# An eight-core encoder layer: token tiles of 384 to 512 in place of 256, and weights cast by DMA into the weight ring

## The chip, the cores and the metric

One Trainium2 chip, all 8 cores. Each core takes two of 16 prompt streams (2 x 2048 tokens) and two of 16 decode streams (2 x 32 tokens); nothing is exchanged between cores. The metric is the device time of the slowest core, in microseconds (us). In some executions the cores of one die, or of both, run at a lower granted clock; such runs are called slow here and are not used for comparisons.

## The reference

One layer: an input projection into six parts, a recurrent branch (conv, gates, scan), a spatial gating branch, a merge with an output projection, and a SwiGLU feed-forward network (FFN). Cut to what matters:

```python
xn = rmsnorm(x, g_pre_mix)
xa, ga, u, v, gates = split(xn @ w_in)            # 1024 -> 6 x 1024
xc, conv_new = causal_conv(xa, conv_prev, conv_w, conv_b)     # width 4
hseq, h_last = rglru(xc, h0, w_a, b_a, w_x, b_x, lam)         # scan over time
o_a = (hseq * gelu(ga)) @ w_br_a
o_b = (gelu(u) * spatial_gate(layernorm(gelu(v)), w_s, b_s)) @ w_br_b
mix = (sigmoid(g_a) * o_a + sigmoid(g_b) * o_b) @ w_out
x   = x + rmsnorm(mix, g_post_mix)
hn  = rmsnorm(x, g_pre_ffn)
gate, up = split(hn @ w_ffn_in)                   # 1024 -> 2 x 2816
x   = x + rmsnorm((silu(gate) * up) @ w_ffn_out, g_post_ffn)
```

## The kernel before

It works in 16 tiles of 256 prompt tokens and one tile of 64 decode tokens. The weights (69 pieces of 128 x 2048) stream through a ring of eight slots, once for each tile. At the start Pool issues casts of the float32 weights into a bfloat16 copy in DRAM, and SP loads the ring from that copy:

```python
TT = 256
...
def rec_cvt(pid):                                  # float32 DRAM -> bfloat16 DRAM
    P.op("pool", lambda e, ...: e.dma_start(out=dst[:, :, c0:c0 + n], in_=src), writes=[("wsc", pid)], ...)
...
    P.op("sp", lambda e, ...: e.dma_start(out=wring[:, slot, :], in_=wsc[pid, :, :]),
         reads=[("wsc", pid)], writes=[("wr", slot)], ...)
```

Mixer and FFN are lists of stages with costs. The FFN of a tile lies 0.35 of a tile behind the next mixer's start, so old FFN work stands beside the start of every mixer. The conv's result, the input of the gates, has a buffer for each of the eight channels:

```python
F_OFFSET = 0.35
...
allst += [(t, 0, i, f) for i, (t, f) in enumerate(timed(mixer_stages(ti), float(ti)))]
allst += [(t, 1, i, f) for i, (t, f) in enumerate(timed(ffn_stages(ti), ti + 1.0 + F_OFFSET))]
...
def s_gate(c):
    P.op("pe", lambda e: e.matmul(ps[:, bg_, 0:ntok], lhsT=wab[:, c, :], rhs=xcb[:, c, 0:ntok], ...),
         reads=[("wab",), ("xcb", c)], ...)
```

Of the kernel before, what the change touches and what calls it, by code (L numbers as in the profile page):

```python
# [6 lines left out]
F32 = mybir.dt.float32  # L7
# [5 lines left out]
D = 1024  # L13
# [6 lines left out]
TT = 256  # L20
NSLOT = 8
CV_AHEAD = 24
INTERLEAVE = True
F_OFFSET = 0.35
FOUT_W = 1.0
# [11 lines left out]

class _Cell:
    __slots__ = ("w", "r")

    def __init__(self):
        self.w = None
        self.r = []

class Prog:
# [47 lines left out]
    def emit(self, block, eng_sems, final_waits):  # L93
        cnt = {e: 0 for e in self.ENGS}
        dcnt = {}
        for e in self.ENGS:
            for o in self.ops[e]:
                if o.dma_sem is not None:
                    k = id(o.dma_sem)
                    dcnt[k] = dcnt.get(k, 0) + 16  # L100
                    o.tok = (o.dma_sem, dcnt[k])
                elif o.needed:
                    cnt[e] += 1
                    o.tok = (eng_sems[e], cnt[e])
        self.final_dma = dcnt
# [31 lines left out]
def build_program(n_prompt_tiles=SEQ // TT, do_sample=True, sample_first=False):  # L137
# [9 lines left out]
    xs_in = din("xs", [2, DEC, D])  # L147
    sh_in = din("sh", [2, D])
    sc_in = din("sc", [2, 3, D])
    g_pre_mix = din("g_pre_mix", [D])  # L150
    w_in = din("w_in", [D, 6 * D])
    conv_w = din("conv_w", [4, D])
    conv_b = din("conv_b", [D])
    w_a = din("w_a", [16, 64, 64])
    b_a = din("b_a", [D])
    w_x = din("w_x", [16, 64, 64])
    b_x = din("b_x", [D])
    lam = din("lam", [D])
    w_br_a = din("w_br_a", [D, D])
    ln_g = din("ln_g", [D])  # L160
    ln_b = din("ln_b", [D])
    w_s = din("w_s", [8, 128, 128])
    b_s = din("b_s", [8, 128])
    w_br_b = din("w_br_b", [D, D])
    w_out = din("w_out", [D, D])
    g_post_mix = din("g_post_mix", [D])
    g_pre_ffn = din("g_pre_ffn", [D])
    w_ffn_in = din("w_ffn_in", [D, 2 * DFF])
    w_ffn_out = din("w_ffn_out", [DFF, D])
    g_post_ffn = din("g_post_ffn", [D])  # L170

    yp = dout("yp", [2, SEQ, D])
    ys = dout("ys", [2, DEC, D])
    hp = dout("hp", [2, D])
    cp = dout("cp", [2, 3, D])
    hs_o = dout("hs", [2, D])
    cs_o = dout("cs", [2, 3, D])
    vs_o = dout("vs", [2, DEC, D])

    pieces = []  # L180

    def add_piece(kc, ncols, srcs):
        pieces.append(dict(kc=kc, ncols=ncols, srcs=srcs))
        return len(pieces) - 1

    def colblk(w, c0, n):
        return w[:, c0:c0 + n].rearrange("(k p) n -> p k n", p=128)

    WIN = [add_piece(8, 256, [(colblk(w_in, cb * 256, 256), 0, 256)]) for cb in range(24)]
    BRA = [add_piece(8, 256, [(colblk(w_br_a, h * 256, 256), 0, 256)]) for h in range(4)]  # L190
    BRB = [add_piece(8, 256, [(colblk(w_br_b, h * 256, 256), 0, 256)]) for h in range(4)]
    WOUT = [add_piece(8, 256, [(colblk(w_out, h * 256, 256), 0, 256)]) for h in range(4)]
    FING = [add_piece(8, 256, [(colblk(w_ffn_in, q * 256, 256), 0, 256)]) for q in range(NFF // 2)]
    FINU = [add_piece(8, 256, [(colblk(w_ffn_in, DFF + q * 256, 256), 0, 256)]) for q in range(NFF // 2)]
    FOUT = [add_piece(2, 1024, [(w_ffn_out[r * 256:(r + 1) * 256, :].rearrange("(k p) n -> p k n", p=128), 0, 1024)])
            for r in range(NFF // 2)]
    NPIECE = len(pieces)
    PSZ = 2048
    wsc = nc.dram_tensor("wsc", [NPIECE, 128, PSZ], BF16).ap()

    tiles = []
    for b in range(2):
        for tt in range(n_prompt_tiles):
            tiles.append(dict(kind="p", b=b, tt=tt, ntok=TT, nsub=TT // 128, PT=128,
                              first=(tt == 0), last=(tt == n_prompt_tiles - 1)))
    if do_sample:
        st = dict(kind="s", ntok=64, nsub=1, PT=64, first=True, last=True)
        if sample_first:
            tiles.insert(0, st)
        else:  # L210
            tiles.append(st)
    NT = len(tiles)

    with contextlib.ExitStack() as es:
# [7 lines left out]
        xbuf = [sb(f"xbuf{i}", [128, 2, D]) for i in range(3)]  # L222
        xsb = [sb(f"xsb{i}", [128, D], BF16) for i in range(2)]
        junk = sb("junk", [128, D], BF16)
        xnTs = [sb(f"xnT{i}", [128, NCH, TT], BF16) for i in range(2)]
        hnT = sb("hnT", [128, NCH, TT], BF16)
        tok = [sb(f"tok{i}", [128, D]) for i in range(2)]
        XAW = TT + 4
        xaT = sb("xaT", [128, NCH, XAW])
        xcf = sb("xcf", [128, NCH, TT])  # L230
        xcb = sb("xcb", [128, NCH, TT], BF16)
        chTr = [sb(f"chTr{i}", [128, TT]) for i in range(2)]
        chTi = [sb(f"chTi{i}", [128, TT]) for i in range(4)]
        chA = [sb(f"chA{i}", [128, TT]) for i in range(4)]
        chE = [sb(f"chE{i}", [128, TT]) for i in range(4)]
        chH = [sb(f"chH{i}", [128, TT]) for i in range(2)]
        gga = sb("gga", [128, NCH, TT])
        hgT = sb("hgT", [128, NCH, TT], BF16)
        gu = sb("gu", [128, NCH, TT])
        gsT = sb("gsT", [128, NCH, TT], BF16)  # L240
        gv = [sb(f"gv{i}", [128, D]) for i in range(2)]
        vn = [sb(f"vn{i}", [128, D], BF16) for i in range(2)]
        Tsig = sb("Tsig", [128, 2, TT])
        t2 = sb("t2", [128, NCH, TT], BF16)
        tmpA2 = sb("tmpA2", [128, 2, TT])
        mixT = sb("mixT", [128, NCH, TT], BF16)
        sgt = [sb(f"sgt{i}", [128, TT]) for i in range(2)]
        ffT = sb("ffT", [128, NFF, TT], BF16)
        hst = sb("hst", [128, NCH, 2])
        stats = sb("stats", [128, 96])  # L250
        st6 = [sb(f"st6_{i}", [128, 4, 6]) for i in range(2)]
        mvt = [sb(f"mvt{i}", [128, 2]) for i in range(2)]
        identf = sb("identf", [128, 128])
        identb = sb("identb", [128, 128], BF16)
        nhalf = sb("nhalf", [128, 1])
        ones128 = sb("ones128", [128, 128], BF16)
        gT_pm = sb("gT_pm", [128, NCH])
        gT_pf = sb("gT_pf", [128, NCH])
        cw = sb("cw", [128, NCH, 4])
        cbT = sb("cbT", [128, NCH])  # L260
        ba2 = sb("ba2", [128, NCH])
        bx2 = sb("bx2", [128, NCH])
        lamT = sb("lamT", [128, NCH])
        cneg = sb("cneg", [128, NCH])
        hcn = sb("hcn", [128, NCH])
        wab = sb("wab", [128, NCH, 128], BF16)
        wxb = sb("wxb", [128, NCH, 128], BF16)
        wsT = sb("wsT", [128, 8, 128], BF16)
        wsS0 = sb("wsS0", [64, 8, 32], BF16)
        wsS1 = sb("wsS1", [64, 8, 32], BF16)  # L270
        bs128 = sb("bs128", [128, 8, 128], BF16)
        gbc_lng = sb("gbc_lng", [128, D])
        gbc_lnb = sb("gbc_lnb", [128, D])
# [5 lines left out]
        psh = ps[:].rearrange("p b (h c) -> p (b h) c", h=2)  # L279

        eng_sems = {e: sem("s_" + e) for e in Prog.ENGS}
        cvt_sems = [sem(f"cv{i}") for i in range(16)]
        ring_sems = [sem(f"rg{i}") for i in range(NSLOT)]
        xl_sems = [sem(f"xl{i}") for i in range(3)]
        y_sems = [sem(f"yo{i}") for i in range(3)]
        c_sems = [sem(f"cst{i}") for i in range(8)]
        so_sem = sem("sto")
        vs_sem = sem("vso")
        block = es.enter_context(nc.Block())

# [4 lines left out]
        stream_log = []  # L295

        def record(P, dry):
            stream = stream_log
            c_ctr = [0]

            def cdma(fn, reads=(), writes=()):
                i = c_ctr[0] % len(c_sems)
                c_ctr[0] += 1
                return P.op("sp", fn, reads=reads, writes=writes, dma_sem=c_sems[i], serial=True)
# [4 lines left out]
            def fb(b):  # L309
                return [("ps", 2 * b), ("ps", 2 * b + 1)]  # L310

            def _touch(b):
                lru.remove(b)
                lru.append(b)

            def alloc_bank():
                for b in lru:
                    if b not in held:
                        _touch(b)
                        return b  # L320
                raise RuntimeError("no free PSUM bank")

            def alloc_half():
                return 2 * alloc_bank()

            def alloc_pair():
                best = None
                for b in range(0, 8, 2):
                    if b in held or (b + 1) in held:
                        continue  # L330
                    age = max(lru.index(b), lru.index(b + 1))
                    if best is None or age < best[0]:
                        best = (age, b)
                if best is None:
                    raise RuntimeError("no free PSUM bank pair")
                b = best[1]
                held.add(b)
                held.add(b + 1)
                _touch(b)
                _touch(b + 1)  # L340
                return b

            def release_pair(b):
                held.discard(b)
                held.discard(b + 1)
                _touch(b)
# [801 lines left out]
```

## Time and profile before

| | before |
|---|---|
| time, median of the first three runs | 2843.87 us (2837.72 to 2921.96) |
| span of the profiled run, slowest core | 2827.5 us |
| one tile of 256 tokens in the middle | 144.1 us (1873 us for 13 tiles) |
| TensorE busy in that stretch | 1706.53 of 1873 us |

PE is TensorE's matmuls, PEld its weight loads, DVE VectorE, ACT ScalarE, POOL GpSimd, SP the core that issues most DMA. The prediction below shows most of the views. Two lines more of the waits of TensorE matter later (what waited, for what, us in all, times, longest): L721 is the gate matmul of before.

```profile
PE ps L721 <- DVE ffT L1033: 32.2, 28, 2.5
...
PE ps L721 <- ACT gga L715: 5.4, 2, 4.4
```

It waits for an FFN block to be done, 1.15 us on average, or for a gelu. The list has no wait of it for its own input, the conv result.

### The profile page before, as it was taken

What the parts mean: (1) busy time and instruction counts of PE and PEld (TensorE: products, weight loads), DVE (VectorE), ACT (ScalarE), POOL (GpSimd) and SP (SyncE); (2) the same over time, 40 slices, a digit from 0 to 9 for tenths busy, and PEclk for the clock granted to TensorE, in tenths of its full rate; (3) what the DMA queues carried; (4) which work ended last, traced back from release to release, by engine and by line L of the source; (5) the groups of instructions that cost most, each with busy time, mean ns of one, the idle gap of its engine ahead of it and who ended that gap; (6) DMA issues with size and microseconds to landing.
All of it is one profiled execution on the core that took longest, in us unless ns stands there. A gap on an engine that the chain in (4) does not pass through costs nothing.

```text
span 2827.5 us, 54756 instructions; the slowest of 8 cores (2805.4 to 2827.5 us)
## 1 busy us (share of the span) xinstructions
PE 2208.4 (78%) x18580; PEld 1756.3 (62%) x18580; DVE 1282.0 (45%) x2588; ACT 1170.9 (41%) x2206; POOL 528.0 (19%) x614
## 2 busy tenths in 40 slices
PE   0041856579899999989989999999989898986585
PEld 0031645358686767676768686767677777774363
DVE  0022432154645455555555555545464646461341
ACT  0052341152636363545445454545353636261421
POOL 2102310220303030303030303030212121211101
PEclk9985977889999999999999999999999999998797
DMA  7997999988888787887778787877878787874787
GB/s 92 156 181 106 243 183 216 189 258 274 271 263 277 252 270 267 274 269 267 264 253 279 252 282 261 274 263 268 276 260 277 252 278 257 281 245 152 242 304 267
DMA packets 264388, 692.41 MB, mean 245 GB/s; under 512 B 41794, under 2 KB 102242, under 8 KB 264116
## 3 DMA queue, kind: packets, MB, share of 16 engines
q1 hardware_dynamic: 200804, 652.72, 69.7%
q0 software_dynamic: 63312, 36.18, 12.3%
q8 instruction: 156, 2.56, 0.4%
q14 instruction: 116, 0.95, 0.1%
HBM read 707.61 MB, written 53.54 MB: 269 GB/s over the span
## 4 chain that ended last, share of the span: by engine, by line
PE 59%; DVE 10%; another core or an unknown queue 9%; DMA 8%; issue 5%; POOL 5%; ACT 3%; SPq 1%; DVEq 0%; POOLq 0%; ACTq 0%
PE ps L1022 22%; PE ps L578 21%; PE ps L1048 8%; DMA wring<-wsc 6%; PE ps L935 4%; PE ps L790 3%; DMA xaT<-sc 2%; DVE xcf L695 1%; POOL stats L417 1%; DVE tok L596 1%; POOL wsc L373 1%; DVE chH L763 1%; DVE chTi L740 1%; POOL gv L818 1%
## 5 line engine op out<-in xcount | busy, mean ns | idle before, releaser
L1022 PE MATMUL ps<-hnT,wring 128*128 128x256 bf16 (+1 forms) x5984 | 712.8, 281 | 126.4 <-DMA wring<-wsc 44.3
L1022 PEld LDWEIGHTS ps<-hnT,wring 128*128 128x128 bf16 x5984 | 586.4, 103 | 227.0 <-issue 140.7
L578 PE MATMUL ps<-xnT,wring 128*128 128x256 bf16 (+1 forms) x5440 | 633.7, 272 | 39.8 <-DVE tok L596 15.5
L578 PEld LDWEIGHTS ps<-xnT,wring 128*128 128x128 bf16 x5440 | 517.9, 100 | 134.5 <-issue 55.5
L1030 DVE SCALAR_TENSOR_TENSOR sgt<-sgt,ps 128x256 f32<-128x256 f32 (+1 forms) x374 | 151.5, 405 | 563.3 <-PE ps L1022 327.6
L1048 PE MATMUL ps<-wring,ffT 128*128 128x512 bf16 (+1 forms) x1452 | 347.0, 388 | 56.0 <-DMA wring<-wsc 49.0
L1028 ACT ACTIVATE sgt<-ps 128x256 f32<-128x256 f32 (+1 forms) x374 | 131.8, 375 | 510.0 <-PE ps L1022 406.9
L1048 PEld LDWEIGHTS ps<-wring,ffT 128*128 128x128 bf16 (+1 forms) x1452 | 142.6, 100 | 213.0 <-issue 77.9
L695 DVE SCALAR_TENSOR_TENSOR xcf<-xaT,cw,xcf 128x256 f32<-128x256 f32 (+1 forms) x408 | 192.8, 473 | 44.1 <-DVE xcf L695 1.9
L414 POOL TENSOR_SCALAR stats<-stats 128x1 f32<-128x1 f32 x165 | 39.1, 237 | 850.2 <-ACT junk L527 572.5
L918 POOL TENSOR_TENSOR mixT<-tmpA,t 128x512 bf16<-128x512 f32 (+1 forms) x68 | 76.3, 1122 | 611.5 <-PE ps L1022 330.3
L527 ACT ACTIVATE junk<-xbuf 128x1024 bf16<-128x1024 f32 (+1 forms) x66 | 69.7, 1056 | 291.5 <-DMA xbuf<-xp 199.2
L935 PE MATMUL ps<-wring,mixT 128*128 128x256 bf16 (+1 forms) x1056 | 132.0, 287 | 52.5 <-POOL mixT L918 49.8
L1033 DVE SCALAR_TENSOR_TENSOR ffT<-sgt,ps 128x256 bf16<-128x256 f32 (+1 forms) x374 | 153.0, 409 | 40.0 <-DVE sgt L1030 1.4
L601 POOL TENSOR_TENSOR xbuf<-xbuf,tok 128x1024 f32<-128x1024 f32 (+1 forms) x66 | 156.4, 2390 | 20.8 <-DVE tok L596 20.8
L706 ACT ACTIVATE xcb<-xcf 128x256 bf16<-128x256 f32 (+1 forms) x136 | 55.2, 406 | 247.9 <-DVE xcf L695 247.8
L935 PEld LDWEIGHTS ps<-wring,mixT 128*128 128x128 bf16 (+1 forms) x1056 | 107.7, 103 | 74.4 <-issue 57.7
L578 PE MATMUL ps<-hgT,wring 128*128 128x256 bf16 (+1 forms) x1088 | 124.9, 268 | 17.3 <-DVE hgT L774 11.8
L790 PE MATMUL ps<-wring,xnT 128*128 128x256 bf16 (+1 forms) x1056 | 128.6, 276 | 12.2 <-DMA wring<-wsc 8.7
L578 PE MATMUL ps<-gsT,wring 128*128 128x256 bf16 (+1 forms) x1088 | 126.4, 270 | 7.2 <-DVE gsT L883 6.3
L691 DVE TENSOR_SCALAR xcf<-xaT,cw,cbT 128x256 f32<-128x256 f32 (+1 forms) x136 | 54.4, 400 | 170.2 <-ACT xaT L686 121.8
L790 PEld LDWEIGHTS ps<-wring,xnT 128*128 128x128 bf16 (+1 forms) x1056 | 104.0, 99 | 40.3 <-issue 16.8
(112 smaller groups left out, 2599.7 us busy)
## 6 DMA issues: line engine op xcount, KB each, us to landing
wring<-wsc SPq DMA_DIRECT2D x1173, 512.0 KB, 5.5
xbuf<-xp SPq DMA_DIRECT2D x16, 1024.0 KB, 7.8
yp<-xbuf SPq DMA_DIRECT2D x32, 512.0 KB, 3.0
wsc<-w_in POOLq DMA_DIRECT2D x24, 512.0 KB, 67.9
wsc<-w_ffn_in POOLq DMA_DIRECT2D x22, 512.0 KB, 84.6
wsc<-w_ffn_out POOLq DMA_DIRECT2D x11, 512.0 KB, 70.9
wsc<-w_br_b POOLq DMA_DIRECT2D x4, 512.0 KB, 63.4
wsc<-w_br_a POOLq DMA_DIRECT2D x4, 512.0 KB, 104.0
```

What stands on the lines that cost most here:

```text
L527: P.op("act", lambda e, src=src, ssc=ssc: e.activation(out=junk[0:PT, :], in_=src, func=AF.Square, accum_out=stats[0:PT, ssc:ssc + 1]), re ...
L578: P.op("pe", lambda e, k=k, m=m: e.matmul(ps[:, b, m * 256:m * 256 + ntok], lhsT=wv[:, k, m * 128:(m + 1) * 128], rhs=rhsT[:, k, 0:ntok], ...
L601: P.op("pool", lambda e: e.tensor_tensor(out=xbuf[xb][0:PT, s, :], in0=xbuf[xb][0:PT, s, :], in1=tok[tk][0:PT, :], op=ALU.add), reads=[("x ...
L695: P.op("dve", lambda e, k=k: e.scalar_tensor_tensor(out=segv(xcf[:, c, :]), in0=xa_win(c, k), scalar=cw[:, c, k:k + 1], in1=segv(xcf[:, c, ...
L790: P.op("pe", lambda e, k=k, bk=bk, s=s: e.matmul(psh[0:PT, bk, 0:256], lhsT=xnT[:, k, s * 128:s * 128 + PT], rhs=wv[:, k, :], start=(k == ...
L918: P.op("pool", lambda e: e.tensor_tensor(out=mixT[:, 2 * mh:2 * mh + 2, 0:ntok], in0=tmpA2[:, :, 0:ntok], in1=t2[:, 2 * mh:2 * mh + 2, 0:n ...
L935: P.op("pe", lambda e, k=k, s=s, bkq=bkq, cq=cq: e.matmul(ps[0:PT, bkq, cq:cq + 256], lhsT=mixT[:, k, s * 128:s * 128 + PT], rhs=wv[:, k, ...
L1022: P.op("pe", lambda e, k=k, m=m, wv_=wv_, jj=jj, b=b: e.matmul(ps[:, b, m * 256:m * 256 + ntok], lhsT=wv_[:, k, jj * 128:(jj + 1) * 128], ...
L1028: P.op("act", lambda e, pv=pv, sg=sg: e.activation(out=sgt[sg][:, 0:ntok], in_=pv[:, 0, :], func=AF.Tanh, scale=0.5), reads=fb(b), writes= ...
L1030: P.op("dve", lambda e, pv=pv, sg=sg: e.scalar_tensor_tensor(out=sgt[sg][:, 0:ntok], in0=sgt[sg][:, 0:ntok], scalar=1.0, in1=pv[:, 0, :], ...
L1033: P.op("dve", lambda e, pv=pv, sg=sg, j=j: e.scalar_tensor_tensor(out=ffT[:, j, 0:ntok], in0=sgt[sg][:, 0:ntok], scalar=0.5, in1=pv[:, 1, ...
L1048: P.op("pe", lambda e, j=j, kk=kk, s=s, half=half: e.matmul(ps[0:PT, prs[s] + half, :], lhsT=ffT[:, j, s * 128:s * 128 + PT], rhs=wv[:, kk ...
```

## The change

The intent: fewer and wider tiles, so that weights are loaded 9 times and not 17, and the decode tokens ride along in the last tile; no serial start, because each float32 piece is cast straight into the ring when it is first wanted, and copied back as bfloat16 from there (half the pieces in tile 0, the others in tile 1). The rewrite replaces most of the file; its core:

```diff
-TT = 256
+def make_tiles():
+    plan = [[4, 4, 4, 4], [4, 3, 3, 3, 3]]          # chunks of 128 tokens; 64 decode tokens join the last
...
+    if pid in cached:
+        P.op("sp", lambda e, ...: e.dma_start(out=wring[:, slot, 0:n], in_=wsc[pid, :, 0:n]), ...)
+        continue
+    P.op("pool", lambda e, ...: e.dma_start(out=wring[:, slot, 0:n], in_=wall[pid, :, 0:n]), ...)   # cast
...
+    if i in todo_wo:                                  # at first use: write back
+        P.op("sp", lambda e: e.dma_start(out=wsc[p_, :, 0:n], in_=wring[:, s_, 0:n]), ...)
...
-allst += [... timed(ffn_stages(ti), ti + 1.0 + F_OFFSET) ...]
+for _, f in pre[:nx["head"]]:                         # next mixer's first projections and conv
+    f()
+for f in merge(pre[nx["head"]:], hnts + F):           # then next mixer and this FFN, merged by cost
+    f()
+for s in range(nx["ns"]):
+    nx["xres"](s)                                     # load x again, for the residual
+tail(t + 1)                                           # branches, output projection, norms: without an FFN beside them
```

In the merged phase a channel of the mixer runs gelu, scan, next conv, gate. The conv result now has two buffers for the channels (`i = rotn("xcb", 2)`), not eight:

```python
for c in range(8):
    add((gc, lambda c=c: s_gelu(c, "ga", gga)))
    if c < 4:
        xa_(c + 4)
    add((0, lambda c=c: s_scan(c)))
    if c < 4:
        conv_(c + 4)
    add((gc, lambda c=c: s_gelu(c, "u", gu)))
    if c < 4:
        add((2 * nt, lambda c=c: s_gate(c + 4)))
    ...
```

## The prediction

> **What bounds the kernel now.** I read the page first (engine shares, slices), then busy time in four stages, the chain of waits of TensorE, the groups by shape, and the timeline at one boundary between mixer and feed-forward (FFN). The page:
>
> ```profile
> span 2827.5 us, 54756 instructions; the slowest of 8 cores (2805.4 to 2827.5 us)
> ...
> PE   0041856579899999989989999999989898986585
> ...
> DMA  7997999988888787887778787877878787874787
> ...
> wsc<-w_in POOLq DMA_DIRECT2D x24, 512.0 KB, 67.9
> ```
>
> TensorE is busy nearly all the time, but only from slice 10 to 35. At the start the DMA engines are full while PE is empty, because the float32 weights are cast from DRAM to DRAM and then loaded. Each cast takes some 68 us to land. At the end there is a hole. The stage table (stretch, length, busy of PE, PEld, DVE, ACT, POOL, clock, DMA share, GB/s) puts sizes to this; 678 and 2551 are the same step of tile 2 and of tile 15:
>
> ```profile
> 0.00:120.00 120.00, 1.94 (x8) 1.57 (x8) 9.07 (x19) 4.21 (x8) 21.94 (x33) 1.00 0.87 127
> 120.00:678.00 558.00, 323.97 (x2538) 251.85 (x2538) 193.28 (x390) 191.21 (x345) 99.72 (x124) 0.83 0.99 199
> 678.00:2551.00 1873.00, 1706.53 (x14273) 1377.12 (x14271) 1001.38 (x1964) 907.92 (x1687) 371.20 (x416) 0.97 0.79 267
> 2551.00:2827.50 276.50, 175.98 (x1767) 125.72 (x1764) 78.25 (x216) 67.55 (x166) 35.11 (x41) 0.81 0.71 242
> ```
>
> The middle is 13 tiles of 256 tokens, so 1873/13 = 144.1 us each. The start wants some 250 us more than its share, and the end holds the decode tile: 64 tokens through all 69 weight pieces. TensorE's waits name the same things, each listed by total us, times and longest us:
>
> ```profile
> PE ps L547 <- ACT xsb L538: 81.8, 1, 81.8
> PE ps L874 <- DVE vn L835: 72.0, 2, 69.0
> PE ps L482 <- DMA gv<-w_s: 68.4, 1, 68.4
> ...
> PE ps L1048 <- DMA wring<-wsc: 49.0, 12, 38.2
> ...
> PE ps L1022 <- DVE hnT L551: 40.1, 11, 15.9
> ```
>
> The first three are start-up, once each. The 38.2 is the decode tile: its sixteen conv-state loads of 1.5 KB sit on the SP queue in front of the weight loads. The last is the norm chain between mixer and FFN, which matters below.
>
> **What the Trainium skill says.** "TensorE: Matmul & The Clock Gate", Back-to-back issue gap: one matmul every N/2.4 + 2.5 ns when warm. The trace agrees: 32 matmuls of 256 columns in 3.66 us against 16 in 1.91 is 109.3 ns each, and 16 of 512 columns in 3.62 us against 8 in 1.89 is 216 ns. So doubling the width saves about 1%. The same section gives 131 ns for N=512 in a stream, which the trace does not show. Same page, Seeing it yourself: a limiter takes a die to 13/16 of the clock once three cores run dense matmuls. This trace does not show it: all eight cores run, and full stretches have clock 1.00. "GPSIMD Engine Reference", Key points: GpSimd shares SBUF interfaces with VectorE when VectorE has two SBUF inputs. The trace agrees: the gate multiply takes 418 ns in the median and up to 2574 beside Pool adds. "DMA: Bandwidth & Descriptors", SWDGE vs HWDGE vs iDMA: a cast has to be issued from GpSimd. The casts here are indeed on POOLq.
>
> **The change, part by part.**
>
> *TensorE work.* A 512-token tile has 816 matmuls with tokens as columns (320 of the input projection, 128 branch, 16 gates, 352 FFN-in) and 4 x 76 = 304 with weights as columns (v 16, output 16, FFN-out 44 per 128 tokens), so 1120 x 0.2157 = 241.6 us. Add 96 spatial and transpose matmuls of 128 columns at 0.056 = 5.4. Total 247.0. With 0.417 ns a column, 384 tokens need 816 x 0.1626 + 228 x 0.2157 + 4 = 185.9 and 448 need 816 x 0.1892 + 304 x 0.2157 + 5.4 = 225.4. The plan is 5 + 3 + 1 tiles: 1235 + 558 + 225 = **2018 us**. The same count for one tile of before is 816 x 0.1093 + 128 x 0.1093 + 88 x 0.2157 + 3.6 = 125.8, times 16 = 2013, plus the decode tile. So the change removes almost no matmul time. What it can remove is everything around it: 18.3 us of idle in each 144.1 us tile (some 293 us), and the start and end.
>
> *DMA.* Ring loads fall from 17 x 69 to 9 x 70 pieces, 512 KB per 250 us x 70 = 147 GB/s against 267. Weights stop being a wait in the steady state. In the first tile all 70 pieces come as 1 MB of float32, cast into the ring, with 35 written back (the other 35 in tile 1). The trace's packet records give 60 ns for a cast packet of 256 elements and 172 ns for one of 1024, so 0.146 ns an element and 321 ns for 2048. Eight such rows per DMA engine make 2.6 us. Ring packets average 195 ns against 159 undisturbed, so I estimate 3.1 us a piece and 1.6 a write-back: 70 x 3.1 + 35 x 1.6 = 273 us, under the 400 us or so that tile 0 takes to the end of its FFN. I add 10 us for local shortages.
>
> *Start.* No 100 us of serial constants: packed vectors, x loaded per 128 tokens, eight casts issued by Pool (0.87 us each), four norms of about 5 us, then 32 small float32 matmuls. First projection at about 40 us. Mixer 0 has no FFN beside it and follows ACT: four gates with table loads (1.28 us each) and two gelus per channel are some 8 us a channel for 8 channels, plus square roots, the channels' last halves and latencies, about 105 us where its matmuls need 59: 46 extra.
>
> *The new boundary.* This is what the change adds. Between mixer and FFN everything is in order: output projection, square (ACT), power (Pool), scale (DVE), add (Pool), square (ACT), power (Pool), scale (ACT), and only then the next tile's first xa copies (ACT), two convs (DVE), a gate, and then the four transposes' multiplies (DVE) that FFN needs. In the kernel before:
>
> ```profile
> 1136.85 1.02 ACT L587 ACTIVATE junk<-ps 128x1024 bf16<-128x1024 f32 x1 [0.43 <-PE ps L935]
> ...
> 1138.46 0.55 POOL L417 TENSOR_TENSOR stats<-stats,nhalf 128x1 f32<-128x1 f32 x1
> ...
> 1140.56 4.67 POOL L601 TENSOR_TENSOR xbuf<-xbuf,tok 128x1024 f32<-128x1024 f32 x2 [0.34 <-DVE tok L596]
> ...
> 1143.06 1.06 ACT L527 ACTIVATE junk<-xbuf 128x1024 bf16<-128x1024 f32 x1 [3.88 <-POOL xbuf L601]
> ...
> 1146.57 2.24 ACT L538 ACTIVATE xsb<-xbuf,stats 128x1024 bf16<-128x1024 f32 x2
> ...
> 1190.35 2.34 DVE L551 TENSOR_TENSOR hnT<-ps,gT_pf 128x1024 bf16<-128x1024 bf16 x2
> ```
>
> Per 128 tokens Pool needs two powers (0.9 each) and an add (2.35) = 4.15 us and ACT 3.35, while the projection delivers one every 3.45. Worked forward in program order, with ACT and Pool waiting for each other, the last scale ends 16.9 us after the last output matmul. Then xa copy 0.6, conv 3.1, conv 3.1, bf16 copy 0.6, two tanh 1.4, gate multiply 1.0, four multiplies 4.7: FFN starts 31.6 us after it. In that time PE has 24 xa matmuls (5.2), a gate (0.4) and transposes (1.8): **24 us of stall**. With 384 tokens the same walk gives 19.5, and for the last tile, without a next one, 17. Before, the old FFN still ran beside this, with a longest wait of 15.9. Sum: 5 x 24 + 3 x 19.5 + 17 = 195. A clock that falls to 0.5 in each stall (0.50 at 1210 to 1214 in the windows of before) costs 3 us nine times: 27.
>
> *The rest.* Inside a merged phase each of the first four channels gives PE 52 matmuls (11.2 us). DVE has a conv, a gate multiply, v's statistics and two FFN blocks (3.1 + 0.9 + 2.9 + 2.8 = 9.7), ACT two table loads, four gate functions and five copies or functions (9.3): close. Later channels have more PE work. I allow 5 us in eight phases: 40. The end, after the last matmul (square, power, multiply, add, store): 17.
>
> *Sum.* 2018 + 40 + 46 + 10 + 195 + 27 + 40 + 17 = 2393 of span. The timed median of before is 16 us above its profiled span (2843.9 against 2827.5), so 2409. I add 11 for stalls I have not seen: **2420 us**, a ratio of 0.85.
>
> **Rivals.** (1) *Fewer weight bytes are the gain.* DMA falls by half, but in the middle PE waits little for it, so this explains the end and the start, not the steady state. If weights were the wait and the boundary were covered by other work, I would get 2393 - 195 - 27 and a few: about 2200. Against it: the DVE order puts the multiplies behind two convs. (2) *ACT and DVE become the bound in merged phases*, as two-deep buffers (xa, gelu, spatial) tie them to PE. Busy shares of 53% and 48% now speak against, in-order engines for. A stall of 3 us per channel makes 8 x 8 x 3 = 190 more: 2600. (3) *The first tile is bound by the cast.* At 5 us a piece (the queue's share of before, 12.3% of 2827.5 us over 69 casts, for small packets) the first tile takes 100 us more: 2510. (4) *Denser matmuls make the chip throttle* to 13/16: 2018/0.8125 is 466 more, so near 2850, no gain. Full clock at 100% busy for 20 us stretches on all cores speaks against; stretches will now be 150 us.
>
> **Range and chances.** The floor of 2018 is firm, and start plus end below 100 is unlikely. Half of the boundary stall missing gives 2310; rivals 2 or 3 in part give 2560. Only rival 4 or two others together keep it above 2787: 4%.
>
> **What would show it.** The profile after should have: matmuls at 216 ns for 512 columns and clock 1.00 in full stretches; first projection near 40 us; tiles of about 285 us; PE waiting some 20 to 25 us once per tile for the normalised FFN input; nearly no wait for ring loads after the second tile; casts near 3 us apart. Wrong would be: no boundary stall, a wait on gate or scan in every channel, casts over 5 us apart, or a clock of 0.81.

## The result, and the profile after

The kernel after is correct. Its six runs: three slow (2788, 2843 and 2861 us) and three fast (2670.36, 2673.42, 2674.43). The median of the six is 2731.46 us; before, run beside it, has a median of 2882.91 (fast runs 2832 to 2844). The ratio of the fast runs is 0.9418, with a 95% interval of 0.9385 to 0.9451. Ratios here are the mean time of one kernel's fast runs over that of the other's of the same rounds, so they are not quite the ratio of the medians quoted. The kernel became faster, as predicted, but both the median and the fast runs lie above the range (2310 to 2560).

The profiled run is a slow one: die 0 is slower and has a lower clock. This is the view by core (span, mean clock):

```profile
core 4: 2652.8 us, clock 0.914
...
die 0 (median of its cores): 2772.5 us, clock 0.853
die 1 (median of its cores): 2658.2 us, clock 0.915
```

What slow means can be read from the clock. This is a stretch of core 0, on die 0 (start and end, length, busy time of five engines with their instructions, clock, DMA share, GB/s):

```profile
800.00:900.00 100.00, 100.00 (x394) 41.97 (x393) 30.98 (x42) 24.65 (x47) 29.16 (x39) 0.81 0.64 208
```

TensorE is busy without a break, at a clock of 0.81. Core 0 spends 1198 us so; the clock record of core 4 holds only 1.00 and 0.50. Some of it occurs in runs that count as fast, too, and is named below where it matters.

All readings of after are therefore taken from core 4, on the undisturbed die. Its page, in 40 slices of 66 us:

```profile
PE   4578699868898698978899699868977886879696
...
DMA  8469699875667243553347244634563454435442
```

The empty slices at the start are gone and DMA is no longer full. But PE, which held 9 and 8 for most of before, now dips to 6 or 7 every four or five slices: once for each tile. In the table by stage (stretch, length, busy of PE, PEld, DVE, ACT and POOL with their instructions, clock, DMA share, GB/s), the marks are the same step of tiles 0, 1 and 8:

```profile
0.00:179.20 179.20, 98.50 (x402) 50.19 (x410) 85.58 (x133) 85.74 (x116) 28.31 (x81) 0.89 0.67 148
...
479.40:2429.70 1950.30, 1632.12 (x8091) 807.30 (x8213) 852.55 (x1318) 790.85 (x1260) 386.97 (x686) 0.92 0.50 159
```

Before had PE busy for 91% of its middle stretch (1706.53 of 1873) at clock 0.97; after has 84% (1632.12 of 1950.30) at 0.92. A 512-token tile takes 300.75 us (1096.64 to 1397.39), more than two tiles of before (288.2). So the steady state became worse, and the whole gain lies at the start and in the decode tokens. The waits of TensorE:

```profile
PE ps L666 <- ACT xcb L659: 263.7, 47, 18.0
PE ps L545 <- ACT ffT L539: 48.0, 8, 15.0
PE ps L977 <- DVE hnT L548: 43.0, 9, 6.2
PE ps L575 <- DMA wring<-wsc: 41.2, 8, 8.9
PE ps L856 <- POOL vnm L833: 12.6, 9, 2.8
```

L666 is the gate matmul, which waits for the bfloat16 copy of a conv result. Listed one by one, its 47 waits fall into three kinds: 7 in the first mixer (34.3 us); 8 at the tile boundaries, of 14.6 to 18.0 us (133.2 us); and 32 in the merged phases, at gates 4 to 7 of each tile from the second on (96.2 us). They last 2.31 to 2.67 us in the first four of these tiles, with 512 tokens, and 1.41 to 11.11 us in the narrower ones. The boundary of tile 3, with what follows it:

```profile
1175.43 5.34 PE L575 MATMUL ps<-xnT,wring 128*128 128x512 bf16 x24
...
1192.67 1.15 ACT L539 ACTIVATE ffT<-x,stats 128x1024 bf16<-128x1024 f32 x1 [1.24 <-POOL hist L610]
...
1198.45 0.59 PE L666 MATMUL ps<-xcb,wab_sb 128*128 128x512 bf16 x1 [17.68 <-ACT xcb L659]
...
1203.20 4.61 DVE L548 TENSOR_TENSOR hnT<-ps,vecs_sb 128x1024 bf16<-128x1024 bf16 x4
...
1208.34 1.06 PE L977 MATMUL ps<-hnT,wring 128*128 128x512 bf16 x2 [5.46 <-DVE hnT L548]
```

The output projection ends at about 1175.4. The last scale of the norm chain ends at 1193.8, the conv follows it, then the gate, then the four multiplies, and the FFN starts at 1208.34. That is 32.9 us after the projection (31.6 predicted), of which PE idles 17.68 + 5.46 = 23.1 (24 predicted).

Now one of the 32 waits in a merged phase:

```profile
1272.93 3.62 PE L977 MATMUL ps<-hnT,wring 128*128 128x512 bf16 x15
1273.17 1.28 DVE L695 TENSOR_TENSOR_SCAN chI<-chA,hst,chI 128x512 f32<-128x512 f32 x1
...
1275.83 2.47 DVE L646 SCALAR_TENSOR_TENSOR xcf<-xa,vecs_sb,xcf 128x512 f32<-128x512 f32 x3
1278.39 0.63 ACT L659 ACTIVATE xcb<-xcf 128x512 bf16<-128x512 f32 x1 [8.00 <-DVE xcf L646]
...
1279.17 0.44 PE L666 MATMUL ps<-xcb,wab_sb 128*128 128x512 bf16 x1 [2.61 <-ACT xcb L659]
...
1280.26 3.13 PE L575 MATMUL ps<-xnT,wring 128*128 128x512 bf16 x8
```

VectorE runs the scan of channel c (0.69 + 1.28 + 0.69 us with its two multiplies) and only then the conv (0.54 + 2.47) that the next gate needs. PE waits 2.61 us. And then eight matmuls take 3.13 us, which take 1.89 at full clock. The stage view shows the clock itself (third number from the end):

```profile
1274.00:1276.00 2.00, 1.95 (x10) 0.92 (x10) 1.78 (x4) 0.00 (x0) 1.17 (x3) 1.00 0.55 203
...
1281.00:1283.00 2.00, 2.00 (x6) 0.69 (x5) 1.95 (x3) 1.97 (x3) 0.00 (x0) 0.56 0.00 0
1283.00:1285.00 2.00, 2.00 (x11) 0.93 (x10) 0.69 (x1) 1.89 (x3) 0.00 (x0) 1.00 0.00 0
```

The clock is 1.00 before the wait, 0.56 after it and 1.00 again from about 1283. Of the 28 such waits of 2.31 us or more, 26 were followed by a low clock; two, of 2.48 and 2.49 us, were not, nor were the four of 1.41 to 1.64 us. A third thing happens once in each output phase. In the timeline of tile 3's:

```profile
1107.43 12.60 SPq L605 DMA_DIRECT2D x<-xp  x4
...
1116.13 0.56 POOL L1054 DMA_DIRECT2D yp<-x  x1 [0.56 <-POOL x L1051]
...
1121.13 3.44 SPq L400 DMA_DIRECT2D wring<-wsc  x4
...
1129.72 2.72 PE L575 MATMUL ps<-xnT,wring 128*128 128x512 bf16 x6 [4.21 <-DMA wring<-wsc]
```

SP issues the four reloads of x (L605) over 12.6 us, because each must wait until the old tile's y, in the same buffer, has been stored. The ring loads behind them in SP's order start only at 1121.13, and PE then waits 4.21 us for weights.

### The profile page after: what moved, and what is told of

Same layout as the page of the kernel before. It is cut to its first block, busy times and chain, and to the rows that moved or that the text cites. A ratio compares the mean times of both kernels' runs of the same rounds, so it can differ in the third digit from the quotient of the medians.

```text
span 2786.9 us, 35362 instructions; the slowest of 8 cores (2649.4 to 2786.9 us)
## 1 busy us (share of the span) xinstructions
PE 2338.8 (84%) x10551; PEld 1108.2 (40%) x10708; DVE 1125.2 (40%) x1716; ACT 1036.8 (37%) x1633; POOL 538.0 (19%) x960
## 4 chain that ended last, share of the span: by engine, by line
PE 67%; DVE 9%; POOL 7%; issue 6%; DMA 6%; ACT 4%; DVEq 0%; POOLq 0%; SPq 0%; ACTq 0%
PE ps L575 22%; PE ps L977 22%; PE ps L1007 12%; PE ps L736 4%; DVE xcf L646 4%; PE ps L856 4%; POOL x L881 2%; DVE chI L695 1%; DMA wring<-wsc 1%; DMA xin<-xp 1%; DVE hnT L548 1%; POOL stats L528 1%; DMA wring<-wall 1%; POOL x L1051 1%; POOL x L1044 1%
## 5 line engine op out<-in xcount | busy, mean ns | idle before, releaser
L977 PE MATMUL ps<-hnT,wring 128*128 128x512 bf16 (+2 forms) x3131 | 728.9, 394 | 50.5 <-DVE hnT L548 43.4
L575 PE MATMUL ps<-xnT,wring 128*128 128x512 bf16 (+2 forms) x2856 | 688.2, 391 | 39.6 <-DMA wring<-wsc 24.7
L977 PEld LDWEIGHTS ps<-hnT,wring 128*128 128x128 bf16 x3168 | 334.4, 106 | 419.8 <-issue 133.7
L575 PEld LDWEIGHTS ps<-xnT,wring 128*128 128x128 bf16 x2880 | 299.8, 105 | 363.9 <-issue 108.7
L666 PE MATMUL ps<-xcb,wab_sb 128*128 128x512 bf16 (+2 forms) x71 | 30.1, 424 | 236.2 <-ACT xcb L659 236.2
L659 ACT ACTIVATE xcb<-xcf 128x512 bf16<-128x512 f32 (+2 forms) x72 | 42.3, 588 | 369.2 <-DVE xcf L646 369.2
L646 DVE SCALAR_TENSOR_TENSOR xcf<-xa,vecs_sb,xcf 128x512 f32<-128x512 f32 (+2 forms) x240 | 156.3, 651 | 27.1 <-DVE xcf L641 0.9
L575 PE MATMUL ps<-gsT,wring 128*128 128x512 bf16 (+2 forms) x571 | 141.0, 395 | 16.7 <-DVE ffT L827 9.1
L991 DVE SCALAR_TENSOR_TENSOR ffT<-sgt,ps 128x512 bf16<-128x512 f32 (+2 forms) x198 | 125.9, 636 | 54.8 <-PE ps L977 40.3
L856 PE MATMUL ps<-wring,vnm 128*128 128x512 bf16 (+1 forms) x515 | 128.2, 412 | 16.2 <-POOL vnm L833 15.7
L575 PE MATMUL ps<-hgT,wring 128*128 128x512 bf16 (+2 forms) x571 | 135.5, 383 | 2.1 <-DMA wring<-wall 1.2
L736 PE MATMUL ps<-wring,xnT 128*128 128x512 bf16 (+1 forms) x500 | 129.4, 410 | 5.3 <-ACT gvf L739 3.3
```

The costliest lines, as they stand in the source:

```text
L575: P.op("pe", lambda e, k=k: e.matmul(ps[:, b, 0:nt], lhsT=wv[:, k, m * 128:(m + 1) * 128], rhs=rhsT[:, k, 0:nt], start=(k == 0), stop=(k = ...
L646: P.op("dve", lambda e, k=k, dst=dst, win=win: e.scalar_tensor_tensor(out=dst, in0=win(k), scalar=vecs[:, V_CW + k, c:c + 1], in1=dst, op0 ...
L736: P.op("pe", lambda e, k=k, wv=wv, b=b: e.matmul(ps[0:PT, b, :], lhsT=xnT[:, k, col:col + PT], rhs=wv[:, k % 4, :], start=(k == 0), stop=( ...
L856: P.op("pe", lambda e, k=k, n=n, wv=wv: e.matmul(ps[0:PT, pr + n, :], lhsT=mixT[:, k, col:col + PT], rhs=wv[:, k % 4, :], start=(k == 0), ...
L977: P.op("pe", lambda e, k=k, wv=wv, b=b: e.matmul(ps[:, b, 0:nt], lhsT=wv[:, k, (j % 2) * 128:(j % 2 + 1) * 128], rhs=hnT[:, k, 0:nt], star ...
L991: P.op("dve", lambda e: e.scalar_tensor_tensor(out=ffT[:, j, 0:nt], in0=sgt[:, i, 0:nt], scalar=0.5, in1=ps[:, bu, 0:nt], op0=ALU.mult, op ...
```

## The experiments

All are edits of the kernel after unless it is said otherwise. Fast runs of after are at 2670 to 2674 us. The first four ran together (before: median 2849.76 of 7), the next four together (2843.02 of 7), the last three on another chip (2854.75 of 7).

### Where the gain lies: without the decode tokens

```diff
-    nc = build_program()
+    nc = build_program(do_sample=False)                       # the kernel before
```
```diff
-            tiles.append(Tile(b, t, n, b == 1 and end, end))
+            tiles.append(Tile(b, t, n, False, end))           # the kernel after
```

Both are wrong: the decode outputs are never written.

> The kernel before, without its decode tile; the sample outputs are left unwritten, so the result is wrong on purpose. Theory A (the gain of the change lies in the start and in the decode tile; the steady state per token got no better, 300 us per 512 tokens after against 288 before): the tile costs what the end of the trace shows beyond one FFN, some 170 to 190 us, so about 2660 us, within 1% of the changed kernel with decode (2670). Rival B (wide tiles and fewer weight bytes gain all along, the decode tile is hidden beside the last FFN): 40 to 60 us less, about 2790.

> The changed kernel without the 64 decode tokens; sample outputs unwritten, wrong on purpose. Theory A: 64 columns more in 816 matmuls cost 0.027 us each (22 us) and a fourth token block 76 x 0.2157 us (16 us), plus longer waits in the last tile: 40 to 60 us less, about 2620. So decode costs 50 inside the last tile against 180 as a tile of its own. Rival B: the same 40, but then the difference between before and after without decode would stay at 150 us or more; theory A says it is 60 or less.

Before without decode: 2691.5 us, ratio 0.9423 (0.9337 to 0.9509). After without decode: 2611.17 us, ratio 0.9135 (0.9052 to 0.9219). The decode tokens cost before 2849.8 - 2691.5 = 158 us and after 2673.4 - 2611.2 = 62 us. So 96 of the some 176 us between the kernels come from where the decode tokens are, and 80 from the prompt part, where a faster start pays for a slower middle. (By the ratios, of different rounds, it is 84 and 82.) Theory A had asked for 60 or less in the prompt part and rival B for 150 or more: the 80 lies between them, nearer to A.

### The conv before the scan

```diff
                     if c < 4:
                         xa_(c + 4)
-                    add((0, lambda c=c: s_scan(c)))
                     if c < 4:
                         conv_(c + 4)
+                    add((0, lambda c=c: s_scan(c)))
```

> One swap in the order of emission: the conv of channel c+4 before the scan of channel c. Theory A: TensorE waits 2.3 us for gates 4 to 7 of each tile because VectorE does the scan (2.65 us) in front of the conv that the gate needs; each such wait also halves the clock for the next few us (1.6 us lost). With the swap these waits fall from about 2.3 to under 0.5 us: 31 x 3.5 = 80 to 110 us less, about 2575. Rival C (VectorE and ScalarE are the bound in this stretch, so the wait moves to another place): within 20 us of the change, waits on the scan or the gelu in its place.

Correct, 2573.93 us, ratio 0.9008 (0.8926 to 0.909). In the fast runs that is 100 us off for two lines exchanged. The same step as above, in its timeline:

```profile
1232.42 3.62 PE L977 MATMUL ps<-hnT,wring 128*128 128x512 bf16 x16
1235.91 0.38 PE L666 MATMUL ps<-xcb,wab_sb 128*128 128x512 bf16 x1
...
1236.56 1.89 PE L575 MATMUL ps<-xnT,wring 128*128 128x512 bf16 x8
```

No wait, and eight matmuls in 1.89 us. In the 512-token tiles all the in-phase gate waits are gone; over all tiles they fall from 96.2 to 22.7 us on core 4, or by 73. The span of core 4 fell by more: from 2652.8 to 2543.2, or by 110. PE's busy time fell too, from 2166.1 to 2132.0 us, for the same matmuls. So some 34 us were the price of the slow clock after these waits: 73 + 34 = 107, of 110 in these two profiles and 100 by the times. The two conv buffers stayed, so the order alone was enough; and VectorE has as much work as before, so it was not the bound that rival C meant.

### Useless matmuls in the waits

```diff
                     br, bi = bank(), bank()
+                    if c >= 4:
+                        for q in range(11):      # results are overwritten
+                            P.op("pe", lambda e: e.matmul(ps[:, br, 0:512], lhsT=wab[:, 0, :], rhs=wsT[:, 0:4, :], start=True, stop=True), ...)
```

> Eleven matmuls without use (2.37 us) into the gate's own PSUM bank in front of gates 4 to 7, where TensorE idles 2.3 us in the changed kernel. Theory A (part of the loss is the clock that drops to half after the short idle): no wait over 1 us is left there, the mean granted clock rises from 0.915 towards 0.935, and 31 x 1.6 = 50 us less, about 2620. Rival D (the idle itself is all of the loss; the clock drop costs nothing more): unchanged within 10 us, or slower where the filler is longer than the wait.

Correct, 2646.54 us, ratio 0.9263 (0.9194 to 0.9332). By the times it is 27 us faster than the fast runs of after; by the two ratios, of different rounds, 0.0155 of some 2840, or 44. Either is less than the 50 expected, but the sign is what counts: TensorE does more work and ends earlier, because work in place of a wait keeps the clock up (0.932 in the median of die 1 against 0.915). On core 4 there are 396 matmuls more, 85 us at 216 ns, but PE's busy time rose by only 57 (2166.1 to 2222.8): the others took 28 us less. The gate waits, at 185.3 us in 26, are as low as with the conv first, yet that kernel is 73 us faster still, since it has no work in their place.

### The FFN's first blocks before the next tile's conv and gate

```diff
-                for _, f in pre[:nx["head"]]:
+                hd = nx["head"]
+                for _, f in pre[:3] + hnts + pre[3:hd - 1] + F[:1] + pre[hd - 1:hd + 2] + F[1:2]:
                     f()
-                for f in merge(pre[nx["head"]:], hnts + F):
+                for f in merge(pre[hd + 2:], F[2:]):
                     f()
```

> Order of emission only: the transposes of the FFN input and the first FFN block stand in front of the next tile's first conv, the second FFN block in front of its first gate. Theory A (the boundary stall of 23 us is the in-order queue of VectorE: conv, conv, gate multiply, then the multiplies FFN needs): FFN starts some 20 us after the last output matmul instead of 33, TensorE's stall falls to about 15 us per tile, 8 boundaries x 8 = 65 us less than the changed kernel, about 2605. Rival E (the stall is the norm chain itself, ScalarE and GpSimd in turn, and the order behind it does not matter): unchanged within 15 us.

Correct, 2575.05 us (2559.29 to 2593.35), ratio 0.9039 (0.8981 to 0.9098): 98 us off, and 30 more than expected. (Its runs are not quite clean: in the profiled one, of 2593 us, every core has 138 to 350 us at a clock of 0.81. The fastest is 114 us off.) On core 4 the waits for the normalised input fell from 43.0 to 12.8 us and those for the gate from 263.7 to 104.6. In their place the transposes now wait for the last scale of the norm chain (137.9 us in 37, from 48.0 in 8): what is left of the boundary is that chain. In sum the waits of the eight boundaries fall from 175 to about 104 us. The gate waits inside the merged phases fall as well, from 96 in 32 to 71 in 27, which theory A did not have.

### The residual's reload later in SP's order

```diff
-                for s in range(nx["ns"]):
-                    nx["xres"](s)
                 tail(t + 1)
...
+                if t > 0:
+                    for s in range(m["ns"]):
+                        extra.setdefault(20, []).append(lambda s=s: m["xres"](s))
```

> The reload of the residual x is issued 20 steps later on the SP queue. Theory A: in the changed kernel the reload waits for the store of y and stands in front of the next x tile and of the weight loads on the same in-order queue, which gives TensorE 4 to 9 us of weight waits and ScalarE a 13 us hole in each output phase. Moved, the weight waits (41 us in 8) fall below 10: 40 to 50 us less, about 2625. Rival F (the weights are late because of DMA bandwidth): the waits stay.

Correct, 2612.19 us (2609.9 to 2613.31), ratio 0.9187 (0.9144 to 0.9231): 61 us off. The wait for ring loads, 41.2 us in 8, is no longer among its waits. It takes more than its own length with it: ScalarE too had waited 13.27 us for the x rows of the next tile behind the same reloads, and the clock fell after these waits as after others. How the remaining 20 us divide between the two was not measured.

### The norm chain: adds on VectorE, and the last scale one step later

```diff
-                        P.op("pool", lambda e, n=n, tk=tk: e.tensor_tensor(out=x1[0:PT, s, n * 512 ...
+                        P.op("dve", lambda e, n=n, tk=tk: e.tensor_tensor(out=x1[0:PT, s, n * 512 ...
...
-                    if i >= 2:
-                        m["hn_a"](i - 2)
-                        m["hn_b"](i - 2)
+                    if 2 <= i <= ns + 1:
+                        m["hn_a"](i - 2)
+                    if i >= 3:
+                        m["hn_b"](i - 3)
```

> In the norm between mixer and FFN the two residual adds go from GpSimd to VectorE and the last scale is emitted one step later, so that ScalarE does not wait for GpSimd each time. Theory A: the last scale ends 9 us after the last output matmul instead of 18, all that hangs on it comes 9 us sooner: 8 x 9 = 70 us less, about 2600. Rival G (the adds only move work to VectorE, which is needed for the convs just then): less than 25 us.

Correct. Three of its five runs are slow (2695.64 to 2852.28); the two fast ones are 2630.28 and 2637.18, a ratio of 0.9264 (0.9195 to 0.9333). That is 40 us off where 70 were expected. The chain itself got shorter as meant: at the boundary of tile 3 on core 4, PE idles 8.53 + 5.08 = 13.6 us and not 23.1. But the cores of its fast profile lie between 2582.7 and 2628.7 us, and the slowest sets the time. Against die 1 of after (2658.2) a core in the middle of them gained some 60 us. The clock tells why they lie so far apart: cores 4 and 5 spent 151 and 144 us at 0.81, the other six none. The slowest of those six is at 2603.1, about 70 us below the fast runs of after, as expected.

### All four together

> The four reorderings together: conv before scan, FFN transposes first, late residual reload, norm chain with adds on VectorE. Theory A: the causes are separate, so the gains nearly add: 97 (measured for the first) + 65 + 45 + 70 = 277, less some 20 that overlap: about 2410. If they are one and the same wait seen in four places, no better than the best two: 2500 or more.

Correct, **2376.14 us** (2374.1 to 2385.14), ratio **0.8364** (0.8321 to 0.8407). This version beats both kernels. Taken alone the four gave 100, 98, 61 and 40 us, in sum 299; together they give 2673.4 - 2376.1 = 297. That these agree is partly luck: FFN first and the norm chain, taken alone, had cores at 0.81; by the readings above they would have given some 114 and 70 without it, and the sum would be 345. So the four act mostly on different losses, with an overlap of some 50 us; FFN first, for one, takes 25 us of the gate waits that the swap takes too. A 512-token tile now takes 262.8 us (802.73 to 1065.54 at the first output matmul), against 247.0 of matmuls. On core 4 the gate waits of after shrink to the first mixer and the last narrow tiles:

```profile
PE ps L545 <- ACT ffT L539: 67.5, 27, 17.0
PE ps L666 <- ACT xcb L659: 59.7, 20, 16.1
```

The first line is the norm chain: 35.3 us of it are the start, 7.2 the last tile, the rest the boundaries. PE is busy for 89 to 90% of the span at a clock of 0.95, on all eight cores.

### Narrow tiles, with after's order and with the new one

```diff
-    plan = [[4, 4, 4, 4], [4, 3, 3, 3, 3]]
+    plan = [[2] * 8, [2] * 8]
```

> The kernel after with sixteen tiles of 256 tokens in place of eight of 384 to 512; casts, write-back, late loads and the decode tokens inside the last tile stay, and so does the order of instructions. If the stalls around each tile's end (about 24 us of boundary for 512 tokens, of which the norm chain's latency is there at any width) are what the time is lost to, twice as many boundaries cost more than the halved conv and scan waits give back: about 2750 us against 2672 for the fast runs of after. If the half of the weight bytes were the gain of the change (rival 1), the narrow tiles would load 17 sets of weights again and the time would come back to 2840 or more. Below 2650 would say that the wide tiles are a loss in themselves.

> The kernel with all four reorderings (conv before scan, FFN first, late residual load, norm chain), with sixteen tiles of 256 tokens in place of eight. With the stalls gone, the wide tile is worth only what it saves in matmul width (1 per cent, about 20 us) and in the few us of boundary that are left, times seven more tiles (about 5 us each, 35 us): I expect about 2430 us against 2376. If weight loading is what wide tiles are for, PE waits for the ring in every tile here and the time is 2550 or more.

After with tiles of 256: 3277.43 us, ratio 1.1477 (1.1391 to 1.1563). With the four reorderings: 2916.58 us, ratio 1.0217 (1.0155 to 1.0278). Both are correct, and both are far above what my theory expected (2750 and 2430). They lie on the rival's side, weight loading, but hundreds of us beyond its line too. The waits of the first, on its slowest core:

```profile
PE ps L666 <- ACT xcb L659: 450.5, 79, 15.3
PE ps L575 <- DMA wring<-wsc: 154.1, 30, 12.2
PE ps L977 <- DVE hnT L548: 52.6, 16, 5.3
```

Listed one by one, a narrow tile has a boundary wait of 14.0 us for the gate and 3.3 for the normalised input, four gate waits that make 14.0, and one of 8 to 12 for the ring: some 41 us in all. A tile of twice the width has 17.4 + 5.5 + 9.3 + 4.2 = 36. I had halved the in-phase waits in thought, but they are the difference between a chain of VectorE work and the PE work beside it, and the PE work halves while much of the chain does not. The second kernel shows what the reordering leaves: 6.9 us at each boundary for the norm chain (130.1 us in 35), 8 in four gate waits, and 147.7 us of ring loads in all (53.3 + 42.3 + 31.2 + 20.9, the casts foremost in the first tiles). So both orders want wide tiles, and the width in itself is worth much more (2916.6 against 2376.1, 540 us) than matmul width. The traces divide the 540, on the slowest cores, as follows: TensorE idles 619.6 us and not 250.2, and is busy 2300.8 and not 2126.0. Of the 369 us more of idle, 142 are waits for ring loads and casts, 91 gate waits, 63 the norm chain and the rest many small ones. Of the 175 us more of busy time, about 128 are slow clock, some 26 of them at 0.81 (busy time times missing clock, added up in windows of 1 us).

### The small set-up matmuls behind the first projections

Edit of the version with all four: the call of the last set-up step (32 float32 matmuls) is moved from before the first mixer to behind its first three projections.

> The kernel with all four reorderings, and the 32 small float32 matmuls of the set-up moved behind the first tile's first three projections. They hold TensorE from about 41.6 to 59 us now. If the first projection is what the start waits for, the end comes some 10 to 18 us earlier: about 2362 us against 2376. If the start is bound by the casts or by ACT (its serial gates and gelus), nothing moves: 2374 to 2378.

Correct, 2385.3 us (2377.99 to 2403.43), ratio 0.8376 (0.8322 to 0.8429): no gain. The first projection now starts at 40.03 us, just where the prediction had it. But on core 1 the first gate is at 67.41, where the version with all four has it at 66.37: the set-up matmuls stand in front of that gate now, so the work was only exchanged. The run does not tell whether removing them would help. Its 9 us over the version with all four are no loss either: cores 0 and 1 spent 158 us at 0.81, and the median of die 1 is 2363.2, against 2368.7 with all four. The 10 to 18 us that were possible by the expectation are not there.

## Why the prediction was wrong

The direction and its reason at large (work is equal, the stalls around it decide) were right. The sum failed by 2652.8 - 2393 = 260 us of span. Step by step, on core 4:

| step of the sum | predicted | measured |
|---|---|---|
| matmul work at full clock | 2018 | not contradicted: 216 ns a matmul of 512 columns, 8 in 1.89 us |
| start (40 + 46) | 86 | 118: the branch matmuls start at 179.2, less some 2 of the next stage and 59 of matmuls |
| boundary stalls | 195 | 190: 133.2 + 42.0 + 15.0 for the last tile |
| gate waits in merged phases | 40 | 96 |
| other waits in the tail | 0 | some 28 |
| ring loads | 10 | 50 (41.2 + 9.2) |
| clock after stalls | 27 | some 113 |
| end | 17 | 25 |

The measured differences add up to 32 - 5 + 56 + 28 + 40 + 86 + 8 = 245 of the 260; 15 are not assigned. The 113 are worked out so: PE's busy time is 2166.1 us in all; less the floor of 2018 and some 17 us of float32 set-up matmuls, 131 us are matmuls that took longer than at full clock; about 18 of them lie in the first 179 us, which the row of the start has already. Busy time times missing clock, in windows of 1 us, gives 106 after the first 179 us.

**The step that failed first** is "I allow 5 us in eight phases: 40". It compared each engine's sum of work in the first four channels (11.2 for PE against 9.7 for VectorE), took "close" for good, and passed over the others with "Later channels have more PE work". Gates 1 to 3 do not wait; all 32 waits are at gates 4 to 7. There VectorE also has the scan, and what decides is the order on it: the scan stood before the conv, so the gate waited, mostly 2.31 us, four times in each tile. The runs showed 96 us there, and exchanging the two steps took 73 of it away.

**The second** is "costs 3 us nine times: 27". I let the clock fall once for each boundary. It fell after most of the 32 gate waits and eight ring waits as well. The mechanism was right and the size was off by a factor of four. The profile of before had a sign of it: the prediction calls 18.3 us of each narrow tile idle, but by its own stage table TensorE idles (1873 - 1706.53)/13 = 12.8, and the other 5.5 are matmuls that took longer than counted. The conv-first run shows 34 us going away with its waits, and the filler run shows the same by putting work in them. How the rest divides between boundaries and other waits was not measured.

**The third** is "I add 10 us for local shortages". I looked at bytes and not at the order of SP's queue. The late-reload run shows what it cost: 61 us with all that hung on it. The start, at 32 us over, is the fourth: the set-up matmuls, which the prediction names but gives no time, moved the first projection from 40 to 58.9 us, and mixer 0 then took 118 us and not 105. Moving them behind the projections gained nothing, so what the start is bound by stays open.

**What was right.** The boundary stall, the largest term that the change adds, was right to 3% and at the step (23.1 us of idle where 24 were predicted). The FFN-first run shows that 71 of its 175 us without the last tile are a matter of order; the rest is the norm chain, which the fourth reordering shortens. Of the other signs that the prediction named, matmuls of 216 ns came too; but a wide tile took 300.75 us and not 285, and one of its signs of being wrong, a wait on the gate, came in half of the channels.

**The rivals.** (1) Fewer weight bytes: in after's order the ring waits are 50 us, so it is no steady-state bound. But the narrow-tile runs speak for it in part, since 154.1 us of ring waits return with 16 sets of loads (the expectation says 17, but the decode tokens have no tile of their own there). (2) VectorE and ScalarE: right that a stall comes from in-order work, with 96 of its 190 us as waits and some 34 in the clock. But neither engine was the bound: the swap took no work away. (3) The cast: wrong; casts land in 9.3 us at the median and PE waits for them for 9.2 us in all. (4) The chip's limiter: not the cause of the miss, since the clock record of core 4 has no 0.81 and the fast runs of after are as slow as core 4. But the clock it names is there: die 0 of the same run has 1163 to 1209 us of it, with 16 matmuls of 512 columns in 4.38 us in place of 3.62.

## What to carry to other kernels

When two chains of work are merged, compare the order on each in-order engine with what TensorE needs next, not the sums of busy time: an engine that is 42% busy held TensorE up 32 times. Expect a wait of over two microseconds to cost again: here 26 of 28 gate waits of 2.31 us or more were followed by some 4 us at little more than half clock. And before tiles are widened, ask which stalls come once for each tile: the four reorderings were worth 297 us on wide tiles and 361 on narrow ones, and still the narrow version was 2% slower than the old kernel.

## What the Trainium skill lacked or had wrong

- "TensorE: Matmul & The Clock Gate", Part 1 (the HAM clock gate) has the clock fall after at least one idle window of about 3.4 us. Here idle times of 2.31 to 2.67 us were mostly enough: after 2.61 us the clock was 0.54 and 0.60 in the next two stretches of 2 us, and eight matmuls took 3.13 us, not 1.89. But after a wait of 3.27 us for the ring it stayed at 1.00. The same page's Back-to-back issue gap gives 131 ns for N=512 in a stream with weight loads; every dense stretch at full clock here shows 216.
- "DMA: Bandwidth & Descriptors", Anatomy of one DMA, says that a semaphore wait happens on the issuing sequencer before dispatch. The runs agree, but the page does not spell out what follows for a ring of weights: a load that waits for a store holds back every load behind it on the same issuing engine. Four reloads held SP for 12.60 us here, and moving them gained 61 us.
